# An MoE encoder block on one core: the branch on the round count is taken directly behind the routing index, ranks are computed one step later, and the final norm is regrouped

## The chip, the cores and the metric

One core of a Trainium2 chip. The metric is device time in microseconds (us), the median of several executions of the whole program; lower is better.

## The reference, cut to what matters

One encoder layer on 1024 tokens of width 1024, all in float32. The first half (norm, projections, differential attention, pooling, output projection) is not touched by the change. The second half is a mixture of experts: a router picks one group of four and two of its eight experts for every token, each of the 32 experts is a gated MLP, and the two weighted results of a token are added, scaled, added to the residual and normed.

```python
x = x + g1 * (mix @ w_out)
h = rms_norm(x, norm2_g) * (1 + sc2) + sh2
g_logits = h @ w_rg + b_rg;  g_sel = top-1 of 4;  g_p = softmax(g_logits)[g_sel]
e_prob = softmax((h @ w_re + b_re)[g_sel]);  top_p, top_i = top_k(e_prob, 2)
weights = g_p * top_p / sum(top_p);  expert_id = g_sel * 8 + top_i
for each expert e, on the tokens whose expert_id is e:
    hid = silu(xb @ w_gate[e]) * (xb @ w_up[e])       # 1024 -> 512
    y[token] += weight * (hid @ w_down[e])            # 512 -> 1024
x = x + g2 * y
return rms_norm(x, final_g)
```

Here 1024 tokens make 2048 assignments to 32 experts, and no expert receives more than 128 of them, so one block of 128 rows per expert is enough for these inputs. The kernel doesn't know this ahead: it counts.

## The kernel before, in words

Tokens are held in T = 8 tiles of 128 rows, one row per partition. Engines work from queues of their own, in program order: what is written earlier in the code for an engine runs earlier, and a waiting instruction holds up all that stands behind it on its engine. SP's queue holds most DMA issues.

**Router steps.** A loop over t = 0 to 8 computes the second part of the output projection of tile t (`out_products`, tiles `pm_0`, and `out_part(t, 4)`, tile `pm_4`; DVE adds both to the residual tile x), and the router of tile t - 1 (`flip` transposes x, `norm2_out` makes the normed rows `xn`, `router` the logits in `plg`). Routing works on batches of tiles (`BATCH`: tiles 0 to 2, 3 and 4, 5 to 7 are batches 0, 1, 2) and is a chain of small DVE instructions, cut in pieces. The tables `PLAN` (behind step t) and `LAST` (behind the loop) say where the pieces stand: `r` one step of `route`, `v` its rest (the weights), `k` `rank` (PE: matmuls `pR` on the one-hot `ob` and its running sums `cums`; DVE: the one-hot slot tiles `pk`), `p` `place` (PE: matmuls `lists`), `n` the norm of the last tile, `w` warm-up matmuls. `EARLY` issues 18 weight loads ahead of the branch, one tile of 128x1024 each.

```python
PLAN = {3: "r0 r0", 4: "r0 v0 k0", 5: "p0 r1 r1", 6: "r1 v1 k1"}
LAST = "p1 w10 r2 n7 r2 r2 k2 w4 p2"
```

**Between router and experts.** DVE turns `lists` into the index `ix`; POOL gathers the rows of the first two experts by it into `XG` (tiles x). `weights()` then finishes the weights of batch 2 (`v2`), places them (`place_weights`, matmuls `wlist`, copied to `LV`), counts the assignments of each expert (`pn`), and DVE makes of the largest the number of extra rounds `nri`. Every engine loads `nri` into a register (`nc.values_load`) and branches over a loop of extra rounds, which is skipped here. `warm2(n)` issues n transposes of the identity on PE whose result nobody reads; two instructions each.

**Experts.** The sequence `seq` holds 32 experts x 12 weight tiles. Each tile is loaded by SP (`w_next`), split by `we_split` into a high part `wh` (ACT) and a low part `wl` (DVE), and used by PE in six matmuls (`pg`, `pu` of the hidden layer, `py` of the result). `AHEAD` = 4 splits run ahead; the first four stand in front of the branch: two in step t = 7, two behind the gathers. `make_x(0, ...)` transposes the gathered rows of the first expert (`px`) and splits them into `xs`, high part on ACT and low part on DVE. ACT needs the table of Silu for the hidden layer (`hx`); it was on another table for Exp.

**End.** The results of the experts are scattered to `yd` in DRAM; SP loads them back as two rows per token (`fy`). `first_sum` adds these two, on DVE for tiles 0 and 1, on POOL for 2 to 7. Then for each tile: PE makes `yp` (sum, and the last expert's rows by a one-hot product; three buffers), DVE multiplies by `g2B` and adds the residual `xf`, ACT squares, POOL makes the reciprocal root `frs`, and DVE scales by it and by the norm row `fgB` (16 matmul rows on PE), and SP stores the tile.

Of the kernel before, what the change touches and what calls it, by code (L numbers as in the profile page):

```python
# [9 lines left out]
F32 = mybir.dt.float32  # L10
# [33 lines left out]
FILL = range(33, 41)  # L44
LOAD_RATE = 2
BATCH = [0, 0, 0, 1, 1, 2, 2, 2]
PLAN = {3: "r0 r0", 4: "r0 v0 k0", 5: "p0 r1 r1", 6: "r1 v1 k1"}
LAST = "p1 w10 r2 n7 r2 r2 k2 w4 p2"
EARLY = {4: 6, 5: 2, 6: 4, 7: 6}
ROWS = [5, 8, 11, 13]  # L50
MODS = {0: 1, 1: 2, 2: 2, **{m: 3 for m in range(3, 12)}}
# [16 lines left out]
def block_kernel(ctx: ExitStack, tc: tile.TileContext, A):  # L68
# [175 lines left out]
    with tc.tile_pool(name="ps0", bufs=2, space=PSUM) as psum, tc.tile_pool(name="ps1", bufs=2, space=PSUM) as psum1, \  # L244
# [790 lines left out]
                    pe.matmul(lists, PK[:, t, k], MV[:, t, k, 0:2].rearrange("p a b -> p (a b)"),  # L1035
                              start=(t0 + t + k == 0), stop=(t0 + t + k == T))

        def place_weights():
            p = pw("wlist", (NE,))
            for c in MVS:  # L1040
                PK, MV = MVS[c]
                t0, nt = RT[c][2:]
                for t in range(nt):
                    for k in range(2):
                        pe.matmul(p, PK[:, t, k], MV[:, t, k, 2], start=(t0 + t + k == 0), stop=(t0 + t + k == T))
                args = mvd[t0:t0 + nt].rearrange("t p k a e -> p t k a e"), MV
                if t0 + nt < T:
                    dma(*args)
                else:
                    stores.append(args)  # L1050
            return p

        pwarm2 = []

        def warm2(n):

# [10 lines left out]
        def plan(what):  # L1067
            for x in what.split():
                c = int(x[1:])
                if x[0] == "r":  # L1070
                    if c not in steps:
                        steps[c] = route(c)
                    next(steps[c], 1)
                elif x[0] == "v":
                    for _ in steps[c]:
                        pass
                elif x[0] == "n":
                    norm2_shift(c, XN.pop(c))
                elif x[0] == "k":
                    rank(c)  # L1080
                elif x[0] == "w":
                    warm2(c)
                else:
                    place(c)

        for t in range(T + 1):
            if t < T:
                out_products(t, 0, (0,))
            if t >= 1:
                flip(t - 1, 0)  # L1090
                flip(t - 1, 1)
                norm2_out(t - 1)
            if t < T:
                out_products(t, 0, (1,))
                out_add(t, 0)
            if t >= 1:
                router(t - 1)
            if t < T - 1:
                out_part(t, 4)
                norm2(t)  # L1100
            elif t == T - 1:
                for g in range(2):
                    we_split(*seq[g])
                out_part(t, 4, (0,))
                out_part(t, 4, (1,))
                norm2(t)
            for _ in range(EARLY.get(t, 0)):
                w_next()
            plan(PLAN.get(t, ""))
        plan(LAST)  # L1110

        dve.tensor_scalar(ix, lists.rearrange("p (a b) -> p a b", a=2), FAR, None, op0=OP.add)
        warm2(9)

        def weights():

            plan("v2")
            dve.tensor_copy(LV, place_weights())
            pn = pw("pn", (NE,))
            pe.matmul(pn, ones_b, cums[:, T], start=True, stop=True)  # L1120
            most = cst.tile([P, 2], F32, name="most")
            nri = cst.tile([P, 1], I32, name="nri")
            dve.tensor_reduce(most[:, 0:1], pn, axis=AX.X, op=OP.max)
            mj = cst.tile([P, 7], F32, name="mj")
            dve.tensor_scalar(mj, bounds, most[:, 0:1], None, op0=OP.is_lt, op1=OP.add, accum_out=most[:, 1:2])
            dve.tensor_copy(nri, most[:, 1:2])
            warm2(14)
            return nri

        XG = [X2[t] for t in (T - 2, T - 1)]  # L1130

        gather(XG[0], ix[:, 0, 0:1])
        gather(XG[1], ix[:, 0, 1:2])
        for g in range(2, AHEAD):
            we_split(*seq[g])
        nri = weights()
        pool_dma(*stores.pop())
        pins.clear()

# [63 lines left out]
    with tc.tile_pool(name="ps5", bufs=2, space=PSUM) as psum, tc.tile_pool(name="ps6", bufs=4, space=PSUM) as psum1:  # L1203
# [62 lines left out]
        def first_sum(t, eng):  # L1266
            eng.tensor_tensor(Y[2 * t], Y[2 * t], Y[2 * t + 1], op=OP.add)

        for step in (0, 2, 1, 3):
            make_x(0, step)  # L1270
        for g, (e, i) in enumerate(seq):
            while len(RW) < min(g + 1 + LOAD, len(seq)):
                w_next()
            if len(RW) == len(seq) and not XF:
                for t in range(T):
                    XF.append(slab(f"xf{t}"))
                    dma(XF[t], x2d[t * P:(t + 1) * P])
                G2.append(slab("g2B"))
                bcast_row(G2[0], rowd[3:4], D)
            if g + AHEAD < len(seq):  # L1280
                we_split(*seq[g + AHEAD])
            products(e, i)
            if i >= 8:
                e += 1
            j = i + 4 * (4 <= i < 8) - 4 * (i >= 8)
            if j == 0:
                if e > 0:
                    hidden(e - 1)
                if e + 2 < NE:
                    gather(XG[e % 2], ix[:, 0, e + 2:e + 3])  # L1290
            if j == HTJ and 0 < e < NE:
                hidden_t(e - 1)
            if j == 4 - (e == 0) and e < NE:
                HS[e] = ring("hx", 1, (512,))
                act.activation(HS[e], PG.pop(e), AF.Silu)
            if j == 8 and e > 0 or j == 7 and e == NE:
                y = ring("y", YN)
                act.activation(y, PY.pop(e - 1), AF.Copy, scale=LV[:, e - 1:e])
                if e < NE:
                    scatter(y, ix[:, 1, e - 1:e])  # L1300
                else:
                    ylast = y
            if (i, e) == (0, 2):
                zero = slab("zero")
                pool.memset(zero, 0.0)
                scatter(zero, ix[:, 1, NE - 1:NE])
            if (i, e) == (0, 3):

                OH.append(slab("onehot"))
                dve.tensor_copy(tlast, ix[:, 0, NE - 1:NE])  # L1310
                pool.iota(OH[0], pattern=[[1, S]], base=0, channel_multiplier=0, allow_small_or_imprecise_dtypes=True)
                pool.tensor_scalar(OH[0], OH[0], tlast, None, op0=OP.is_equal)
            if i == 4 and e == NE - 1:

                for t in range(T):
                    for k in range(2):
                        Y.append(slab(f"fy{t}_{k}"))
                        dma(Y[-1], yd.rearrange("(t k) d -> k t d", k=2)[k, t * P:(t + 1) * P])
            if i == 8 and e == NE:
                for t in range(2):  # L1320
                    first_sum(t, dve)
                for t in range(2, 5):
                    first_sum(t, pool)
            if j == 11 and e == NE - 1:
                hidden(e)
                hidden_t(e)
            if e + 1 < NE and j in (X_AT if e else X_AT0):
                make_x(e + 1, (X_AT if e else X_AT0)[j])
# [1 line left out]

    g2B = G2[0]
    psum = ctx.enter_context(tc.tile_pool(name="ps8", bufs=3, space=PSUM))
    fgB = rows(psum.tile([P, D], F32, name="fgB", bufs=1), fg)
    SS, RF, YP = {}, {}, {}
    for t in range(-1, T + 2):
        if 5 <= t + 4 < T:
            first_sum(t + 4, pool)
        if t + 1 < T:
            p = YP[t + 1] = psum.tile([P, 2, 512], F32, name=f"yp{t + 1}", tag="yp")
            for h in range(2):  # L1340
                cs = slice(h * 512, (h + 1) * 512)
                pe.matmul(p[:, h], ident, Y[2 * t + 2][:, cs], start=True, stop=False)
                pe.matmul(p[:, h], OH[0][:, (t + 1) * P:(t + 2) * P], ylast[:, cs], start=False, stop=True)
        if 0 <= t < T:
            y0, y1 = Y[2 * t:2 * t + 2]
            dve.tensor_tensor(y0, YP.pop(t).rearrange("p a b -> p (a b)"), g2B, op=OP.mult)
            dve.tensor_tensor(y0, y0, XF[t], op=OP.add)
            SS[t] = sm("fss", (1,))
            act.activation(y1, y0, AF.Square, accum_out=SS[t])
        if 0 <= t - 1 < T:  # L1350
            RF[t - 1] = sm("frs", (1,))
            rsqrt(RF[t - 1], SS[t - 1], 1, 1.0 / D, "fr")
        if 0 <= t - 2 < T:
            y0, y1 = Y[2 * t - 4:2 * t - 2]
            dve.scalar_tensor_tensor(y1, y0, RF[t - 2], fgB, op0=OP.mult, op1=OP.mult)
            dma(out[(t - 2) * P:(t - 1) * P], y1)

# [80 lines left out]
```

## Time and profile before

| | us |
|---|---|
| median of 3 runs (lowest to highest) | 1154.58 (1154.49 to 1155.22) |
| profiled execution, device time | 1156.02 |
| its span (first to last instruction) | 1154.2 |
| busy: PE, DVE, ACT, POOL | 1095.3, 971.5, 728.2, 248.6 |
| router steps t = 0 to 8 and placing, up to `ix` | about 444 to 519.5 |
| `ix` to the first matmul of the first expert | 519.5 to 534.4 |
| experts | 534.4 to 1108.2 |
| end | 1108.2 to 1154.2 |

Times of the stretches are of the profiled execution. A timeline row gives an instruction's (or a run of like instructions') start, length, engine, line, operation, output<-input, and in brackets the idle time of its engine ahead of it with what ended it. All helpers record their line as L81, so rows are told apart by the names of tiles.

### The profile page before, as it was taken

What the parts mean: (1) busy time and instruction counts of PE and PEld (TensorE: products, weight loads), DVE (VectorE), ACT (ScalarE), POOL (GpSimd) and SP (SyncE); (2) the same over time, 40 slices, a digit from 0 to 9 for tenths busy, and PEclk for the clock granted to TensorE, in tenths of its full rate; (3) what the DMA queues carried; (4) which work ended last, traced back from release to release, by engine and by line L of the source; (5) the groups of instructions that cost most, each with busy time, mean ns of one, the idle gap of its engine ahead of it and who ended that gap; (6) DMA issues with size and microseconds to landing.
All of it is one profiled execution on the core that took longest, in us unless ns stands there. A gap on an engine that the chain in (4) does not pass through costs nothing.

```text
span 1154.2 us, 15871 instructions
## 1 busy us (share of the span) xinstructions
PE 1095.3 (95%) x5379; PEld 899.1 (78%) x5379; DVE 971.5 (84%) x1232; ACT 728.2 (63%) x932; POOL 248.6 (22%) x197
## 2 busy tenths in 40 slices
PE   5898998999999999889999999999999999999984
PEld 5687787778888778778888888888888888888851
DVE  6977787689998766775999999999999999999957
ACT  6641232388877002224888888888888888888812
POOL 1000000178888011101131110110111101101042
PEclk9899999999999999978999999999999999999997
DMA  9949699696836435437999999999999999999473
GB/s 366 382 147 379 213 340 353 263 251 158 195 117 251 198 136 211 175 116 281 409 388 379 385 386 386 388 391 382 390 377 385 387 382 382 388 378 385 191 297 146
DMA packets 103719, 349.62 MB, mean 303 GB/s; under 512 B 16754, under 2 KB 17682, under 8 KB 103634
## 3 DMA queue, kind: packets, MB, share of 16 engines
q1 hardware_dynamic: 92034, 323.08, 76.3%
q0 software_dynamic: 11456, 24.96, 5.6%
q8 instruction: 43, 0.70, 0.3%
q10 hardware_dynamic: 144, 0.52, 0.1%
q14 instruction: 42, 0.34, 0.1%
HBM read 309.95 MB, written 55.33 MB: 316 GB/s over the span
## 4 chain that ended last, share of the span: by engine, by line
PE 48%; DVE 2%; issue 1%; DMA 1%; ACT 0%; SPq 0%; DVEq 0%; ACTq 0%
PE pg L81 28%; PE py L81 15%; PE px L81 2%; DVE fy L81 1%; PE pht L81 1%; DMA we<-in_w_exp 1%; PE yp L81 1%; DVE wl L81 1%; ACT wh L81 0%; SPq L102 0%; PE fgB L81 0%; ACT y L81 0%; DVE hx L81 0%; DVEq L1436 0%; ACT fy L81 0%
## 5 line engine op out<-in xcount | busy, mean ns | idle before, releaser
L81 DVE TENSOR_TENSOR wl<-we,wh 128x1024 fp32r<-128x1024 f32 x384 | 458.6, 1222 | 39.9 <-ACT wh L81 33.0
L81 ACT ACTIVATE wh<-we 128x1024 fp32r<-128x1024 f32 x384 | 399.9, 1059 | 58.7 <-PE pg L81 29.1
L81 PE MATMUL pg<-wh,xs 128*128 128x512 f32 x1024 | 338.7, 397 | 1.6 <-ACT xs L81 1.6
L81 PEld LDWEIGHTS pg<-wh,xs 128*128 128x128 f32 x1024 | 193.1, 189 | 40.5 <-ACT xs L81 1.8
L81 PE MATMUL pg<-wl,xs 128*128 128x512 f32 x512 | 200.3, 391 | 0.0
L81 PE MATMUL py<-wh,hth 128*128 128x512 f32 x512 | 172.3, 398 | 1.1 <-ACT hth L81 0.7
L81 POOL DMA_INDIRECT yd<-y,ix x31 | 30.8, 995 | 442.1 <-ACT y L81 441.8
L81 PEld LDWEIGHTS py<-wh,hth 128*128 128x128 f32 x512 | 96.8, 189 | 21.5 <-DVE hth L81 1.0
L81 PEld LDWEIGHTS pg<-wl,xs 128*128 128x128 f32 x512 | 96.8, 189 | 18.3
L81 PE MATMUL py<-wl,hth 128*128 128x512 f32 x256 | 100.5, 393 | 0.0
L81 ACT ACTIVATE e<-s,mx 128x1024 f32<-128x1024 f32 x64 | 71.8, 1121 | 28.8 <-DVE mx L81 25.1
L81 DVE TENSOR_REDUCE mx<-s 128x1 f32<-128x1024 f32 x64 | 78.2, 1222 | 6.0 <-PE s L81 3.2
L81 PE MATMUL s<-k,sq 128*128 128x512 f32 x256 | 72.6, 405 | 5.1 <-ACT e L81 5.0
L81 POOL TENSOR_TENSOR e<-e,e 128x1024 f32<-128x1024 f32 x32 | 76.6, 2393 | 2.7
L81 PE MATMUL po<-wh,v 128*128 128x256 f32 x256 | 60.8, 302 | 0.0
L81 POOL DMA_INDIRECT x<-xnd,ix x32 | 48.0, 1499 | 55.9 <-PE px L81 34.6
L81 DVE SCALAR_TENSOR_TENSOR wt<-wt,cB 128x1024 f32<-128x1024 f32 x48 | 56.3, 1219 | 0.8 <-ACT cB L81 0.8
L81 POOL TENSOR_SCALAR e<-e,cc 128x1024 f32<-128x1024 f32 x32 | 39.3, 1229 | 81.3 <-DVE cc L81 71.1
L81 PEld LDWEIGHTS py<-wl,hth 128*128 128x128 f32 x256 | 48.6, 190 | 9.5
L81 DVE SCALAR_TENSOR_TENSOR x<-pm,Y,x 128x1024 f32<-128x1024 f32 (+1 forms) x33 | 41.3, 1251 | 16.6 <-PE pm L81 15.5
L81 PEld LDWEIGHTS s<-k,sq 128*128 128x128 f32 x256 | 44.1, 189 | 13.8 <-ACT e L81 7.2
L81 ACT ACTIVATE xn<-x 128x1024 f32<-128x1024 f32 x7 | 7.4, 1061 | 70.4 <-DVE x L81 44.5
(246 smaller groups left out, 1864.7 us busy)
## 6 DMA issues: line engine op xcount, KB each, us to landing
we<-in_w_exp SPq DMA_DIRECT2D x384, 512.0 KB
wt<-in_w_ada SPq DMA_DIRECT2D x48, 512.0 KB
win<-in_w_in SPq DMA_DIRECT2D x16, 512.0 KB
woB<-wod SPq DMA_DIRECT2D x16, 512.0 KB
fy<-yd SPq DMA_DIRECT2D x16, 512.0 KB
k<-kd SPq DMA_DIRECT2D x32, 192.0 KB
xt<-in_xT SPq DMA_DIRECT2D x8, 512.0 KB
wo<-in_w_out SPq DMA_DIRECT2D x8, 512.0 KB
```

Source lines behind the costliest of these rows:

```text
L81: ins = getattr(self.eng, op)(*args, **kw)
```

## The change

Four things. (1) `PLAN` and `LAST`: `k0` moves from the end of step 4 to the head of what follows step 5, `p0` from there to step 6, `v1 k1` from the end of step 6 to step 7, ahead of `out_part(7, 4)`; there they take the place of the first two weight splits, which move to the ends of steps 5 and 6. The count `pn` (`c0`) stands ahead of `p2`. (2) The round count (`most`, `mj`, `nri`) stands directly behind `ix`; `v2`, the nine warm-up passes, `wlist` and `LV` follow, and then comes the branch. The fourteen warm-up passes behind `pn` are gone, and the third and fourth weight split stand behind the branch. (3) A Silu of one column (`tlast<-one`, overwritten later) stands behind the branch in the code. (4) End: DVE makes the first sums of tiles 0 to 3, POOL those of 4 to 7; `fgB` stands between `yp` of tiles 1 and 2; the last tile is scaled and stored in two halves, the second from ACT's queue.

```diff
-PLAN = {3: "r0 r0", 4: "r0 v0 k0", 5: "p0 r1 r1", 6: "r1 v1 k1"}
-LAST = "p1 w10 r2 n7 r2 r2 k2 w4 p2"
+PLAN = {3: "r0 r0", 4: "r0 v0", 5: "k0 r1", 6: "p0 r1 r1", 7: "v1 k1"}
+LAST = "p1 w10 r2 n7 r2 r2 k2 w4 c0 p2"
...
+                elif x[0] == "c":
+                    CP.append(pw("pn", (NE,)))
+                    pe.matmul(CP[0], ones_b, cums[:, T], start=True, stop=True)
...
             elif t == T - 1:
-                for g in range(2):
-                    we_split(*seq[g])
+                plan(PLAN[t])
                 out_part(t, 4, (0,))
                 out_part(t, 4, (1,))
                 norm2(t)
             for _ in range(EARLY.get(t, 0)):
                 w_next()
-            plan(PLAN.get(t, ""))
+            if t < T - 1:
+                plan(PLAN.get(t, ""))
+            if t in (5, 6):
+                we_split(*seq[t - 5])
         plan(LAST)
         dve.tensor_scalar(ix, lists.rearrange("p (a b) -> p a b", a=2), FAR, None, op0=OP.add)
-        warm2(9)
-        def weights():
-            plan("v2")
-            dve.tensor_copy(LV, place_weights())
-            pn = pw("pn", (NE,))
-            pe.matmul(pn, ones_b, cums[:, T], start=True, stop=True)
-            ...
-            warm2(14)
-            return nri
         XG = [X2[t] for t in (T - 2, T - 1)]
         gather(XG[0], ix[:, 0, 0:1])
         gather(XG[1], ix[:, 0, 1:2])
-        for g in range(2, AHEAD):
-            we_split(*seq[g])
-        nri = weights()
+        ...
+        dve.tensor_reduce(most[:, 0:1], CP[0], axis=AX.X, op=OP.max)
+        dve.tensor_scalar(mj, bounds, most[:, 0:1], None, op0=OP.is_lt, op1=OP.add, accum_out=most[:, 1:2])
+        dve.tensor_copy(nri, most[:, 1:2])
+        plan("v2")
+        warm2(9)
+        wl = pw("wlist", (NE,))
+        place_weights(wl)
+        dve.tensor_copy(LV, wl)
         pool_dma(*stores.pop())
...
+        act.activation(tlast, one, AF.Silu)
+        for g in range(2, AHEAD):
+            we_split(*seq[g])
         for step in (0, 2, 1, 3):
             make_x(0, step)
...
-                for t in range(2):
+                for t in range(3):
                     first_sum(t, dve)
-                for t in range(2, 5):
+                for t in range(4, 6):
                     first_sum(t, pool)
...
-    fgB = rows(psum.tile([P, D], F32, name="fgB", bufs=1), fg)
     for t in range(-1, T + 2):
-        if 5 <= t + 4 < T:
-            first_sum(t + 4, pool)
+        if t == -1:
+            first_sum(3, dve)
+        if 6 <= t + 5 < T:
+            first_sum(t + 5, pool)
...
+            if t == 0:
+                fgB = rows(psum.tile([P, D], F32, name="fgB", bufs=1), fg)
```

On DVE, between the index and the branch, the order before was as follows (`rt` and `mv` are the pieces of `v2`; `wl` are the third and fourth split; the last row loads the register that the branch reads):

```order
L81 TENSOR_SCALAR ix<-lists 128x64
L81 TENSOR_TENSOR wl_4646<-we_2_4215,wh_4645 128x1024
L81 TENSOR_TENSOR wl_4650<-we_3_4217,wh_4649 128x1024
L81 TENSOR_REDUCE rt_4399<-rt_4399 128x3 x2
...
L81 TENSOR_TENSOR mv<-rt_4399 128x6x32
L81 COPY LV<-wlist 128x32
L81 TENSOR_REDUCE most<-pn 128x1
L81 TENSOR_SCALAR mj,most<-bounds,most 128x7
L81 CAST nri<-most 128x1
L1141 TENSOR_LOAD nri
```

The same place on DVE now:

```order
L81 TENSOR_SCALAR ix<-lists 128x64
L81 TENSOR_REDUCE most<-pn 128x1
L81 TENSOR_SCALAR mj,most<-bounds,most 128x7
L81 CAST nri<-most 128x1
L81 TENSOR_REDUCE rt_4388<-rt_4388 128x3 x2
...
L81 TENSOR_TENSOR mv<-rt_4388 128x6x32
L81 COPY LV<-wlist 128x32
L1135 TENSOR_LOAD nri
```

The two splits went behind the branch, where they stand ahead of the two low parts `xs`; the count went ahead of `v2`.

On ACT, from the gathers' side of the branch to the first weight split of the stream, the order before was (rows of the skipped loop left out):

```order
L81 ACTIVATE wh_4645<-we_2_4215 128x1024
L81 ACTIVATE wh_4649<-we_3_4217 128x1024
L1141 TENSOR_LOAD nri
L1143 COMPARE_AND_BRANCH
...
L81 ACT_TABLE_LOAD
L81 ACTIVATE xs_4894<-px_0_4884 128x512
L81 ACTIVATE xs_4897<-px_1_4889 128x512
```

and it is now:

```order
L1135 TENSOR_LOAD nri
L81 ACT_TABLE_LOAD
L81 ACTIVATE tlast<-one 128x1
L1137 COMPARE_AND_BRANCH
...
L81 ACTIVATE wh_4863<-we_2_4215 128x1024
L81 ACTIVATE wh_4867<-we_3_4217 128x1024
L81 ACTIVATE xs_4881<-px_0_4871 128x512
L81 ACTIVATE xs_4884<-px_1_4876 128x512
```

The table load, with the one-column Silu, is now ahead of the branch instruction itself, although its line stands behind the branch in the code; two weight splits stand between the branch and `xs`. A second table load, ahead of the first `hx`, is gone too.

On DVE in steps 6 and 7 (`xn` the normed rows of tiles 5 and 6, `x` the residual adds of tile 7, `rt`, `mv`, `pk` the pieces of `v1` and `k1`) the end of the stretch is now:

```order
L81 TENSOR_TENSOR mv<-rt_4194,tok_104 128x4x64
L81 TENSOR_TENSOR wl_4437<-we_1_4213,wh_4436 128x1024
L81 SCALAR_TENSOR_TENSOR xn_4398<-x_3491,RS,gB 128x1024
L81 TENSOR_TENSOR xn_4398<-xn_4398,shB 128x1024
L81 TENSOR_TENSOR x_3493<-pm_0_4440,x_3493 128x1024
L81 SCALAR_TENSOR_TENSOR rt_4388<-plg,RS,rbias 128x36
L81 TENSOR_REDUCE rt_4194<-rt_4194 128x2 x2
...
L81 TENSOR_TENSOR pk_4499<-slots,RK 128x256 x2
L81 SCALAR_TENSOR_TENSOR x_3493<-pm_4_4509,Y_253,x_3493 128x512 x2
```

Before, `v1` and `k1` stood where the split `wl_4437` stands here, ahead of `xn`, and both first splits stood where `rt` to `pk` stand here.

## Rows read from the trace of the kernel before

**Rows 1.** Windows, expert stage: busy of each engine, granted clock, DMA share, GB/s.
```profile
559.00:584.00 25.00, 25.00 (x119) 20.73 (x118) 22.95 (x23) 21.82 (x24) 7.07 (x6) 1.00 1.02 406
```

**Rows 2.** Waits in 464.2 to 505: us in total, times, longest.
```profile
DVE x L81 <- PE pm L81: 9.0, 7, 2.7
...
PE pR L81 <- DVE ob L81: 3.9, 2, 2.0
...
DVE rt L81 <- PE plg L81: 1.4, 3, 0.5
```

**Rows 3.** Windows of DVE alone: busy, granted PE clock, DMA share, GB/s.
```profile
464.20:505.00 40.80, 29.35 (x75) 0.90 0.48 167
```

**Rows 4.** Timeline of DVE in steps 5 to 7.
```profile
476.82 1.28 DVE L81 SCALAR_TENSOR_TENSOR x<-pm,Y,x 128x1024 f32<-128x1024 f32 x1 [1.20 <-PE pm L81]
...
499.94 2.35 DVE L81 TENSOR_TENSOR wl<-we,wh 128x1024 fp32r<-128x1024 f32 x2
...
504.23 0.75 DVE L81 SCALAR_TENSOR_TENSOR x<-pm,Y,x 128x512 f32<-128x512 f32 x1 [1.28 <-PE pm L81]
```

**Rows 5.** Timeline of PE from the index to the first expert.
```profile
521.18 4.26 PE L81 MATMUL wlist<-mv,pk 128*128 128x32 f32 x32
...
525.30 6.02 PE L81 MATMUL pwarm<-ident 128*128 128x128 f32 x28
531.73 1.06 PE L81 MATMUL px<-ident,x 128*128 128x128 f32 x8 [0.40 <-PEq L1143]
534.37 0.79 PE L81 MATMUL pg<-wh,xs 128*128 128x512 f32 x1 [1.58 <-ACT xs L81]
...
535.39 1.05 PE L81 MATMUL pg<-wh,xs 128*128 128x512 f32 x2
```

**Rows 6.** Timeline of DVE over the same stretch.
```profile
525.47 0.19 DVE L81 COPY LV<-wlist 128x32 f32<-128x32 f32 x1 [2.24 <-PE pn L81]
...
526.06 0.15 DVE L81 CAST nri<-most 128x1 int32<-128x1 f32 x1
534.35 1.29 DVE L81 TENSOR_TENSOR xs<-px,xs 128x512 fp32r<-128x512 f32 x2 [8.13 <-ACT xs L81]
```

**Rows 7.** The branch's line: durations in ns, first and last start in us.
```profile
L1143 DVEq EVENT_SEMAPHORE  x1: 21/21/21, 527.1 to 527.1; - x1
...
L1143 PEldq EVENT_SEMAPHORE  x1: 51/51/51, 531.4 to 531.4; - x1
```

**Rows 8.** Timeline of ACT behind the branch.
```profile
532.42 1.28 ACT L81 ACT_TABLE_LOAD   x1 [17.07 <-PE px L81]
533.72 1.09 ACT L81 ACTIVATE xs<-px 128x512 fp32r<-128x512 f32 x2
```

**Rows 9.** DMA issues in 519 to 529: KB each, median us to landing.
```profile
x<-xnd,ix POOLq DMA_INDIRECT x2, 4.7
```

**Rows 10.** Timeline of POOL: first gather.
```profile
519.83 1.84 POOL L81 DMA_INDIRECT x<-xnd,ix  x1 [12.75 <-DVE ix L81]
```

**Rows 11.** Windows with the granted clock (third column from the right).
```profile
534.00:538.00 4.00, 3.63 (x9) 2.87 (x10) 2.52 (x3) 2.42 (x4) 0.11 (x1) 0.57 1.02 398
538.00:542.00 4.00, 4.00 (x20) 3.27 (x19) 3.03 (x3) 3.11 (x4) 0.00 (x0) 1.00 1.02 412
...
524.00:531.00 7.00, 7.00 (x36) 7.00 (x36) 0.67 (x5) 0.00 (x0) 0.37 (x1) 0.51 0.46 149
```

**Rows 12.** Timeline of the end: PE, POOL and DVE.
```profile
1109.39 2.05 PE L81 MATMUL fgB<-ident,cols 128*128 128x128 f32 x16 [1.20 <-ACT y L81]
...
1112.39 2.35 POOL L81 TENSOR_TENSOR fy<-fy,fy 128x1024 f32<-128x1024 f32 x1 [0.21 <-DMA fy<-yd]
...
1114.97 1.22 DVE L81 TENSOR_TENSOR fy<-yp,g2B 128x1024 f32<-128x1024 f32 x1 [6.53 <-PE yp L81]
1116.23 2.22 DVE L81 TENSOR_TENSOR fy<-fy,xf 128x1024 f32<-128x1024 f32 x1
...
1146.00 2.46 DVE L81 SCALAR_TENSOR_TENSOR fy<-fy,frs,fgB 128x1024 f32<-128x1024 f32 x2
```

More of the change, by code (lines that the diff above doesn't have):

```diff
@@ L1036, in place, with place_weights @@
                               start=(t0 + t + k == 0), stop=(t0 + t + k == T))
-        def place_weights():
-            p = pw("wlist", (NE,))
+        def place_weights(p):
             for c in MVS:
@@ L1050, in place_weights @@
                     stores.append(args)
-            return p
-        pwarm2 = []
+        pwarm2, CP = [], []
         def warm2(n):
@@ L1108, in block_kernel @@
                 w_next()
-            plan(PLAN.get(t, ""))
+            if t < T - 1:
+                plan(PLAN.get(t, ""))
+            if t in (5, 6):
+                we_split(*seq[t - 5])
         plan(LAST)
         dve.tensor_scalar(ix, lists.rearrange("p (a b) -> p a b", a=2), FAR, None, op0=OP.add)
-        warm2(9)
-        def weights():
-            plan("v2")
-            dve.tensor_copy(LV, place_weights())
-            pn = pw("pn", (NE,))
-            pe.matmul(pn, ones_b, cums[:, T], start=True, stop=True)
[L1121 to L1126, printed above, removed]
-            warm2(14)
-            return nri
         XG = [X2[t] for t in (T - 2, T - 1)]
@@ L1133, in block_kernel @@
         gather(XG[1], ix[:, 0, 1:2])
-        for g in range(2, AHEAD):
-            we_split(*seq[g])
-        nri = weights()
+        most = cst.tile([P, 2], F32, name="most")
+        nri = cst.tile([P, 1], I32, name="nri")
+        dve.tensor_reduce(most[:, 0:1], CP[0], axis=AX.X, op=OP.max)
+        mj = cst.tile([P, 7], F32, name="mj")
+        dve.tensor_scalar(mj, bounds, most[:, 0:1], None, op0=OP.is_lt, op1=OP.add, accum_out=most[:, 1:2])
[5 more added lines that the diff above has]
+        dve.tensor_copy(LV, wl)
         pool_dma(*stores.pop())
@@ L1354, in block_kernel @@
             y0, y1 = Y[2 * t - 4:2 * t - 2]
-            dve.scalar_tensor_tensor(y1, y0, RF[t - 2], fgB, op0=OP.mult, op1=OP.mult)
-            dma(out[(t - 2) * P:(t - 1) * P], y1)
+            for h in range(2 if t - 2 == T - 1 else 1):
+                cs = slice(h * 512, (h + 1) * 512) if t - 2 == T - 1 else slice(0, D)
+                dve.scalar_tensor_tensor(y1[:, cs], y0[:, cs], RF[t - 2], fgB[:, cs], op0=OP.mult, op1=OP.mult)
+                (act_dma if h else dma)(out[(t - 2) * P:(t - 1) * P, cs], y1[:, cs])
 def _layouts(inp):
```

## Prediction

> **What bounds the kernel now.** I read the windows of the expert stage first: a window of 25.00 us there has PE busy for 25.00 us at granted clock 1.00 [rows 1]. PE sets the pace from the first expert's matmul at 534.37 [rows 5] to the end of the experts, and 18 weight tiles lie loaded ahead of the branch by the table in the code. So whatever brings the first expert's matmuls forward brings the end forward by as much, and what happens on ACT, DVE or SP inside the experts is covered by PE. The change touches three stretches around this block: router steps, branch, end. They follow each other, so their terms add.
>
> In the router steps the waits tell who is late. Between 464.2 and 505 DVE is busy for 29.35 us of 40.80 [rows 3]; it waits 9.0 us in seven waits for PE's `pm`, and 1.4 us for `plg`. PE, in turn, stands still twice, 3.9 us in all, because `pR` needs `ob` of a routing step that DVE has only just begun [rows 2]. Neither engine is full: each waits for the other in turn.
>
> Around the branch the timelines show two late parties. DVE has copied `LV` at 525.66 and written `nri` at 526.21 [rows 6], and is through the branch at 527.1 [rows 7]. PE has 28 warm-up instructions queued, 6.02 us from 525.30 [rows 5], and passes only at 531.4 [rows 7]. Then `px`, a table load of 1.28 us on ACT ahead of `xs` [rows 8], the first expert's `pg` at 534.37, and its third matmul pair, the first that uses the low part of `xs`, at 535.39 [rows 5].
>
> **Router steps: 6.0 us.** No DVE instruction is added or dropped between the residual add of tile 4 and the last add of tile 7 (504.98 [rows 4]); they change places. What can shrink is the idle time, 40.80 - 29.35 = 11.45 us [rows 3]: 10.4 us of named waits [rows 2] and 1.05 us of gaps. With `k0` a step later, PE goes on with the matmuls of tile 5 while DVE finishes batch 0; with `k1` behind tile 6's products the same holds for batch 1. Walking DVE's new order by these durations, PE runs ahead of it nearly throughout, and these waits stay: the one for `pm` behind the router row of step 5, as at 476.82 (1.20); that for the second half of the last tile, as at 504.23 (1.28) [rows 4]; and a new one. The first weight split now stands behind routing steps whose Exp runs on ACT, and its `wl` has to wait until ACT has made `wh`: 1024 columns take 1.09 us there [rows 8], I take 1.35 us with the hand-over. With the gaps and 0.5 us for `plg` that leaves 1.20 + 1.28 + 1.35 + 1.05 + 0.5 = 5.4 us idle, so a gain of 6.0. Bounds: if all three `plg` waits (1.4) and one more wait of 1.20 stay, 4.0 (11.45 - 7.5); if the new wait and that for `plg` don't arise, 7.9. The moved splits (2.35 us for two [rows 4]) cost nothing extra, since they stand in the same stretch before and after. Behind 504.98 nothing but the count `pn` (one small matmul) is added up to `ix`, so the gain arrives there whole.
>
> **Branch: 5.5 us.** All times here are on before's clock. DVE now writes `nri` right behind `ix`, which nothing waits for; it then finishes `v2` without the two splits ahead of it. PE still does nine warm-up passes and `wlist`, until 525.44 [rows 5]: this set the time of `LV` before and does so now, so `LV` ends at 525.66. From its last instruction to passing, DVE took 527.1 - 526.21 = 0.9 us [rows 6, 7], so it is through at 526.55. PE has no warm-up passes left and is through earlier, but `px` waits for the others' release: about 526.75. ACT loaded its table ahead of the branch, where it idles for 17.07 us [rows 8], so `xs` starts 0.69 us behind `px` (532.42 - 531.73 [rows 5, 8]), at 527.45, and `pg` could start near 528.1. But DVE now has the third and fourth split first: 526.55 + 2.35 = 528.9 [rows 4], and half of 1.29 us [rows 6] for the low part of `xs`: 529.55. That is what the third pair waits for: about 529.65 to 529.9 instead of 535.39 [rows 5]. I take 5.5. So 1.5 us of what PE and ACT give free is spent on the two splits; if they found cover, the gain would be 7.0. The first gather is issued at 519.83 [rows 10] and lands 4.7 us later [rows 9], at 524.5, ahead of `px` by 2.2 us: the cover holds, but it was 7 us before. The low bound is 4.5, with 1 us lost to such landings. SP's weight loads restart earlier too; 18 loaded tiles cover them either way. The Silu's own column and the second table load cost PE nothing [rows 1].
>
> What the warm-up passes might have bought is the clock. Rows say: 0.51 in 524 to 531, while they ran, and 0.57 in 534 to 538, behind them; 1.00 from 538 [rows 11]. So the first expert started at half speed with them, and I charge nothing for their absence.
>
> The Trainium skill, "TensorE: Matmul & The Clock Gate", Part 1, says that the throttled state is the default and that activity releases it; by that, dropping the passes would cost the first expert clock. That speaks against this edit. Rows 11 show that the passes had not released it, and the effect is among the rivals below.
>
> **End: 0.75 us.** DVE sums tile 3 as soon as it lands (1112.39, where POOL's sum starts now [rows 12]) in about 1.2 us, and multiplies at 1113.6 instead of 1114.97, since PE's `yp0` no longer stands behind `fgB`'s 2.05 us [rows 12]. That is 1.3 us at best. Against it, the residual add takes 2.22 us while POOL adds [rows 12], and POOL still has four sums to do in that time; and `fgB` now delays `yp` of tile 2. I take 0.75, between 0 and 1.3. The halved last tile (the two last scalings take 2.46 us from 1146.00 [rows 12]) could bring its first half out by 0.6 us, but the store of tile 6 is ahead of it on the same DMA engines: 0 to 0.3, taken as 0.
>
> **Sum.** 6.0 + 5.5 + 0.75 = 12.25 us. Against the profiled execution: 1156.02 - 12.25 = 1143.8; it lies 1.44 above the median of the runs, so on that scale 1154.58 - 12.25 = 1142.3.
>
> **Rivals.**
> *A: the warm-up passes covered something that is now bare.* Behind PE's late pass at 531.4 any late arrival between 526.5 and 531 cost nothing: code of the block behind the branch, a landing, another engine's release. The nearest price for a fetch from memory is a DMA's 4.7 us [rows 9]. Then the branch gives 0.8 and the time is 1147.0. Against it: DVE's 0.9 us holds register load, comparison and jump [rows 6, 7], which leaves little for a stall.
>
> The Trainium skill, "Runtime: NRT & Kernel Launch", Instruction fetch mechanics, has the rule behind this: a taken branch to a page outside the two in the fetch window stalls until a DMA has brought it. By that rule each engine pays at the skipped loop; DVE's 0.9 us here shows no such stall, but PE's and ACT's could hide before 531.4.
>
> *B: the router is not freed.* If DVE's waits move to other partners (ACT's `wh` ahead of each `wl`, POOL's share of the norm), only about 2 us of the 11.45 go: 2 + 5.5 + 0.75, or 1146.3. For it: the seven waits for `pm` are spread over the stretch, the longest 2.7 us [rows 2], and are not only the sequel of two stops. Against it: a PE that never stops for `ob` is 3.9 us further on [rows 2] and has the products ready.
>
> *C: slower, by the clock.* If PE without the passes stays at half clock in the experts, each us so spent loses 0.5 us of work. The gain is gone once this lasts 24.5 us longer than before, and beyond 29 us the time is over 1156.9. Against it: PE is busy without a pause from 538 on and the clock came to 1.00 within 4 us of its start [rows 11]; PE will not be less busy then.
>
> *D: more than I count.* Splits under cover (7.0) and the router at 7.9: 1138.4.
>
> **How the numbers follow.** Forecast, 1140.2 to 1144.6 around 1142.3: 0.65. A (1144.6 to 1149): 0.13. B (1144.6 to 1148.3): 0.13. D: 0.05. C or an unseen loss: 0.04, most of it ending near no change. A measurement of this kernel can tell about 0.2%, 2.3 us, from no change. Faster by more than that: forecast, D and nearly all of A and B, 0.94; within: 0.03; slower: 0.03. The range takes in the forecast and most of A, B and D: 1139.5 to 1147.0.
>
> **What would show it.** Router right: the `pR` waits for `ob` gone, DVE idle in the stretch near 5.4 us, `wl` waiting once for `wh`. Branch right: PE passes near `wlist`'s end, no table load behind the branch, `pg`'s third pair some 10 us after `LV` was due to 4 us after, waiting for DVE's `xs`. End right: `fy<-yp` of tile 0 some 1.3 us earlier relative to ACT's last `y`. Wrong, if granted clock stays at 0.5 beyond the first 4 us of the experts, if `px` waits for its gather, or if DVE or ACT starts its first instruction behind the branch more than 1 us after its comparison.

## The result, and the profile after

| | us |
|---|---|
| changed kernel, median of 5 runs (lowest to highest) | 1146.33 (1144.31 to 1148.30) |
| ratio to the kernel before, with its 95% interval | 0.9924 [0.9903, 0.9945] |
| the same as a difference (of 1155) | 8.8 less (6.4 to 11.2) |
| profiled execution of the changed kernel: time, span | 1144.32, 1142.3 |
| predicted: median, range; on the profile's scale | 1142.3, 1139.5 to 1147.0; 1143.8 |

One of before's five runs beside these took 1245.93 us, where the others took 1154.49 to 1155.84; it is in a slow state and stands outside the ratio.

The time lies in the range and went the way that was forecast, but the gain is 8.8 us and not 12.25; the forecast's own band, 1140.2 to 1144.6, was missed. The two profiled executions alone differ by 1156.02 - 1144.32 = 11.7 us, almost as forecast. So the mechanism has to be looked for in the traces, and the missing 3.4 us in what the profile of before was.

The waits in the changed router steps, with the total, how often, and the longest:

```profile
DVE x L81 <- PE pm L81: 3.4, 3, 1.7
...
PE pm L81 <- DVE x L81: 3.2, 1, 3.2
...
DVE wl L81 <- ACT wh L81: 1.2, 1, 1.2
```

PE no longer waits for `ob` (3.9 us [rows 2]). DVE's waits for `pm` fell from 9.0 to 3.4 us, and the new wait for `wh` is there, once, with 1.2 us. One stop of PE stays, for DVE's first half of the last tile (`x`): 2.50 us before, 3.2 us now. DVE alone over the stretch, from the residual add of tile 4 to the end of tile 7's last add:

```profile
464.88:500.46 35.58, 30.02 (x75) 0.94 0.60 203
```

It is idle for 35.58 - 30.02 = 5.56 us; the prediction left 5.4. The parts differ more than the sum: the waits for `pm` are 3.4 us where it had 1.20 + 1.28, and none for `plg` falls into the stretch, where it had 0.5. From the index to the first expert, PE's timeline:

```profile
514.59 2.23 PE L81 MATMUL pwarm<-ident 128*128 128x128 f32 x18
516.65 3.78 PE L81 MATMUL wlist<-mv,pk 128*128 128x32 f32 x32
521.93 1.94 PE L81 MATMUL px<-ident,x 128*128 128x128 f32 x8 [1.50 <-DVEq L1137]
523.75 0.80 PE L81 MATMUL pg<-wh,xs 128*128 128x512 f32 x1
...
524.88 0.79 PE L81 MATMUL pg<-wh,xs 128*128 128x512 f32 x1
```

`px` starts 6.91 us behind the end of `ix` (515.02) where the prediction had 7.2, and the third pair 9.86 us, where it had 10.1 to 10.4; before it was 15.85 [rows 5]. The wait ahead of `px` is for DVE's way through the branch (duration in ns, first and last start in us):

```profile
L1137 PEldq EVENT_SEMAPHORE  x1: 51/51/51, 520.5 to 520.5; - x1
L1137 DVEq COMPARE_BRANCH  x1: 72/72/72, 521.1 to 521.1; - x1
L1137 DVEq EVENT_SEMAPHORE  x1: 21/21/21, 521.7 to 521.7; - x1
```

PE is through at 520.5, DVE at 521.7: `LV` ended at 520.66, so DVE needed 1.04 us (0.9 was reckoned). What differs from the plan is PE's speed: the eight `px` take 1.94 us where they took 1.06 [rows 5]. The windows show the clock that goes with it (granted clock in the third column from the right):

```profile
519.00:523.00 4.00, 2.50 (x17) 2.40 (x17) 1.33 (x2) 1.19 (x2) 0.00 (x0) 0.63 0.62 197
523.00:527.00 4.00, 4.00 (x12) 2.70 (x11) 3.65 (x5) 2.15 (x4) 1.04 (x1) 0.52 0.95 335
527.00:531.00 4.00, 4.00 (x19) 3.25 (x18) 2.58 (x3) 3.18 (x3) 0.00 (x0) 1.00 1.02 391
```

At the end DVE multiplies 4.27 us behind ACT's last `y` (1098.24) instead of 5.63, and pays part of it back at tile 2, behind the norm row:

```profile
1101.37 1.22 DVE L81 TENSOR_TENSOR fy<-fy,fy 128x1024 f32<-128x1024 f32 x1 [1.36 <-DMA fy<-yd]
1102.51 1.22 DVE L81 TENSOR_TENSOR fy<-yp,g2B 128x1024 f32<-128x1024 f32 x1
...
1110.68 1.22 DVE L81 TENSOR_TENSOR fy<-yp,g2B 128x1024 f32<-128x1024 f32 x1 [2.33 <-PE yp L81]
1111.94 1.96 DVE L81 TENSOR_TENSOR fy<-fy,xf 128x1024 f32<-128x1024 f32 x1
```

### The profile page after: what moved, and what is told of

Its sections match the earlier page's. It is cut to its first block, busy times and chain, and to the rows that moved or that the text cites. A ratio compares the mean times of both kernels' runs of the same rounds, so it can differ in the third digit from the quotient of the medians.

```text
span 1142.3 us, 15812 instructions
## 1 busy us (share of the span) xinstructions
PE 1091.3 (96%) x5351; PEld 895.7 (78%) x5351; DVE 971.2 (85%) x1235; ACT 726.7 (64%) x932; POOL 245.7 (22%) x195
## 4 chain that ended last, share of the span: by engine, by line
PE 49%; DVE 2%; DMA 2%; issue 0%; ACT 0%; POOL 0%; SPq 0%; DVEq 0%; ACTq 0%
PE pg L81 30%; PE py L81 15%; PE px L81 3%; DMA fy<-yd 2%; DVE fy L81 2%; PE pht L81 1%; DVE wl L81 0%; ACT wh L81 0%; SPq L102 0%; POOL frs L81 0%; ACT fy L81 0%; POOL fy L81 0%; DVEq L1440 0%; DVE hx L81 0%; ACT y L81 0%
## 5 line engine op out<-in xcount | busy, mean ns | idle before, releaser
L81 DVE SCALAR_TENSOR_TENSOR x<-pm,Y,x 128x1024 f32<-128x1024 f32 (+1 forms) x33 | 41.3, 1251 | 15.9 <-PE pm L81 14.8
```

Source lines behind the costliest of these rows:

```text
L81: ins = getattr(self.eng, op)(*args, **kw)
```

## The experiments

Two questions: does each of the three terms show when its part is built alone, and why is the measured gain smaller than the one between the two profiles? Theory 1 is the prediction's: three terms that add, sized as there. Its rivals in the first four runs are that a gain moves on into another wait, that missing passes cost clock, and that runs differ by the clock at the start (theory S). Theory L came out of these four: the old order's own length varies with the clock, and the profile of the prediction had the long ones. Each kernel left one more profile, and four stretches can be read in each from the timelines of DVE, PE and ACT: R, from the start of tile 4's last residual add to the end of tile 7's; B, from the end of `ix` to PE's third `pg` pair; X, from there to the end of ACT's last `y`; E, from there to the start of the two last scalings. "Start" is where R begins; all code ahead of it is the same in all kernels. From R's end to `ix` all kernels take 14.5 to 14.8 us.

| | start | R | B | X | E |
|---|---|---|---|---|---|
| before (profile of the prediction) | 463.00 | 41.98 | 15.85 | 573.95 | 36.66 |
| e9, before again | 466.76 | 40.15 | 13.93 | 572.97 | 36.94 |
| e1, router part alone | 463.35 | 35.58 | 13.93 | 572.91 | 36.13 |
| e2, branch part alone | 465.00 | 38.51 | 9.56 | 573.95 | 37.34 |
| e3, end part alone | 467.24 | 40.10 | 13.94 | 572.99 | 35.61 |
| e5, before, stops filled | 467.07 | 39.50 | 14.01 | 572.99 | 36.86 |
| changed kernel | 464.88 | 35.58 | 9.86 | 573.36 | 35.81 |
| e4, changed kernel again | 463.99 | 35.57 | 11.71 | 573.19 | 36.26 |
| e6, changed, fourteen passes back | 468.80 | 35.12 | 14.80 | 570.98 | 37.02 |
| e7, changed, splits ahead | 465.85 | 35.57 | 9.37 | 573.65 | 36.06 |
| e8, changed, no passes behind `ix` | 465.61 | 35.58 | 9.24 | 572.16 | 35.90 |
| e10, changed, no Silu | 465.50 | 35.58 | 9.80 | 574.50 | 35.93 |
| e11, e8 with another end | 464.17 | 35.58 | 8.81 | 572.78 | 36.20 |
| e12, e11 with splits ahead | 467.16 | 35.57 | 8.78 | 572.29 | 35.98 |

**e1: the router part alone.**

```diff
-PLAN = {3: "r0 r0", 4: "r0 v0 k0", 5: "p0 r1 r1", 6: "r1 v1 k1"}
+PLAN = {3: "r0 r0", 4: "r0 v0", 5: "k0 r1", 6: "p0 r1 r1", 7: "v1 k1"}
...
+                plan(PLAN[t])
...
+            if t in (5, 6):
+                we_split(*seq[t - 5])
```

> Before, with the table of steps of the change alone (ranks one step later, first two splits in steps 5 and 6). Theory 1 (the terms add, each as in the prediction): 6 us less than before; from the residual add of tile 4 to the end of the last add of tile 7 some 35.6 us instead of 41.98; the branch as before, with pg's third pair some 15.8 us behind the index. Theory 2 (the gain comes only because the later parts are also changed, and waits move on otherwise): under 3 us, with PE or DVE waiting longer between the last add of tile 7 and the index than the 14.56 us that both kernels took. If runs of one kernel differ by the clock at the start of the program, the profile's first 42 us show it.

Ratio 0.9951 [0.9928, 0.9973], 5.7 us less. R is 35.58, as theory 1 said and as in the whole change to 0.01 us; B is 13.93, which neither theory had (15.8): the branch of this kernel is that of before, word for word. So 15.85 wasn't the branch's own length. Theory 2 is out: from R's end to `ix` it takes 14.54 us, as before.

**e2: the branch part alone** (early count, `v2`, nine passes, `wlist`, `LV`, branch; splits and Silu behind it).

> Before, with the early round count, no fourteen warm-up passes, two splits and the Silu behind the branch; steps and end as before. Theory 1: 5.5 to 6 us less than before, pg's third pair some 9.9 us behind the index instead of 15.85, router steps as before (41.98 us). Theory 2 (without the passes the experts run longer at half clock): 2 to 4 us less, with granted clock near 0.5 in the experts for longer than the 3 to 4 us behind the first pg that before shows.

Ratio 0.9953 [0.9933, 0.9972], 5.4 us less. B is 9.56, near theory 1's 9.9. Theory 2's half clock is there, at 0.50 from 526.5 to 530.5, hardly longer than the 3 to 4 us that it allowed before. But R, the router of before, takes 38.51 instead of 41.98. PE's runs of twelve `pm` behind the two stops show where that comes from; in this kernel:

```profile
467.41 2.99 PE L81 MATMUL pm<-woB,mu 128*128 128x512 f32 x12
...
490.19 2.98 PE L81 MATMUL pm<-woB,mu 128*128 128x512 f32 x12
```

In the profile of before both took 4.6 us behind the same stops of 2.0 and 1.9 us; its timeline of PE:

```profile
465.42 4.58 PE L81 MATMUL pm<-woB,mu 128*128 128x512 f32 x12
...
489.80 4.60 PE L81 MATMUL pm<-woB,mu 128*128 128x512 f32 x12
```

The granted clock from 489.80 to 494.20 was 0.61 there. Over the four profiles with before's router (before, e2, e3, e9) four of eight such runs took 4.6 us and four 3.0; R is 38.51 with none, 40.10 and 40.15 with one, 41.98 with two. With the new order these two stops are gone, and R is 35.6 in every profile but e6 (35.1). Why the same stop has full clock behind it in one execution and half clock in another, the traces don't show.

**e3: the end alone.**

> Before, with the regrouped end alone. Theory 1: 0.5 to 1.2 us less, inside what times can tell; from ACT's last y to the last scaling 0.8 us less than before, because yp of tile 0 starts 2 us earlier and then yp of tile 2 waits for the norm row. Rival: POOL's sums delay DVE's residual adds as before, and nothing is gained (0 to 0.3 us).

Ratio 0.9996 [0.9973, 1.0018]: not to be told from before, as expected of 0.8 us. In the profile E is 35.61, below the 36.13 to 37.34 of the five with the old end. That speaks against the rival (nothing); the times don't rule it out.

**e4: the changed kernel again.**

> The changed kernel as it is. Theory 1: the sum of the three parts, some 11 to 12 us less than before; if single runs spread over 4 us again, theory S (start): the profile's first 42 us, which the change doesn't touch, show granted clock between 0.65 and 0.85 and explain the spread by up to 2 us. Rival: the spread arises in the branch or the experts' first us, and the runs of e1 and e3 have none of it.

1144.83 (1142.38 to 1147.84), ratio 0.9920 [0.9891, 0.9948]: 9.2 us. Theory S holds in part. Over 22 to 42 us, in code that the change doesn't touch, the granted clock is 0.67 in the first profile of the changed kernel and 0.82 here. The changed kernel:

```profile
22.00:42.00 20.00, 15.70 (x53) 12.31 (x53) 17.10 (x22) 12.81 (x17) 0.09 (x1) 0.67 1.03 409
```

and again (e4):

```profile
22.00:42.00 20.00, 14.48 (x60) 11.26 (x59) 18.37 (x24) 14.29 (x19) 0.00 (x0) 0.82 1.03 409
```

Here R starts 0.9 us earlier. Its rival holds as well: B is 11.71 instead of 9.86, since the nine passes ran at half clock this time. PE's timeline of e4:

```profile
513.77 4.00 PE L81 MATMUL pwarm<-ident 128*128 128x128 f32 x18
517.61 3.88 PE L81 MATMUL wlist<-mv,pk 128*128 128x32 f32 x32
523.00 1.94 PE L81 MATMUL px<-ident,x 128*128 128x128 f32 x8 [1.50 <-DVEq L1137]
```

**e5: before, with PE's two stops filled.**

```diff
+PLAN = {3: "r0 r0", 4: "w9 r0 v0 k0", 5: "p0 r1 r1", 6: "w9 r1 v1 k1"}
```

> Before, with nine warm-up passes on PE ahead of each of the first two ranks, where PE stands still for about 2 us. Theory L (the router's gain has a fixed part and one that hangs on the clock: behind a stop the twelve pm matmuls take 4.6 or 3.0 us, by execution): no stop, no slow run of twelve, and from the residual add of tile 4 to the end of tile 7's last add 38.5 to 39 us. Theory 1 (the stops themselves, each 2 us of idle PE, make the stretch long, whatever the clock): 41 to 42 us as in the profile of before, since the passes fill the time but DVE is as late as before.

Ratio 0.9981 [0.9960, 1.0002]. R is 39.50, between the two; theory 1's 41 to 42 is out, and neither dozen of `pm` takes 4.6 us:

```profile
466.87 2.17 PE L81 MATMUL pwarm<-ident 128*128 128x128 f32 x18
...
469.48 2.98 PE L81 MATMUL pm<-woB,mu 128*128 128x512 f32 x12
...
492.56 2.98 PE L81 MATMUL pm<-woB,mu 128*128 128x512 f32 x12
```

The 1.0 us over e2's 38.51 isn't spent on the passes: the first `pR` starts 1.97 us behind the start of R in both kernels. Some 0.3 us arise in step 6 between `lists` and `pm`, and 0.7 us at the last tile, where PE stops for DVE in every kernel and nothing was filled; the first matmuls behind that stop took 0.72 us in e2 and here

```profile
504.13 1.22 PE L81 MATMUL pm<-woB,mxh 128*128 128x512 f32 x2 [2.50 <-DVE x L81]
```

Since the twelve matmuls behind a stop took 4.6 us in half the cases only, two of 2.98 us prove little by themselves; they agree with theory L.

**e6: the changed kernel with the fourteen passes put back.**

```diff
         dve.tensor_copy(LV, wl)
+        warm2(14)
```

> The changed kernel with the fourteen warm-up passes put back behind the copy of the weights, ahead of the branch. If the passes cost what the prediction says and buy no clock: pg's third pair 3 to 6 us later behind the index than the 9.6 to 9.9 us (one profile: 11.7) without them, by the clock at which the passes run (28 instructions take 3.5 us at full and 6 us at half clock), and the experts behind it no shorter than 573 us from there to ACT's last y. Rival (they buy clock): the experts 1 to 2 us shorter, so that half of it comes back.

Ratio 0.9939 [0.9924, 0.9955], by time not to be told from the changed kernel. B is 14.80 and X is 570.98. PE's timeline of e6:

```profile
518.27 4.15 PE L81 MATMUL pwarm<-ident 128*128 128x128 f32 x18
...
526.06 5.00 PE L81 MATMUL pwarm<-ident 128*128 128x128 f32 x28
531.46 1.07 PE L81 MATMUL px<-ident,x 128*128 128x128 f32 x8 [0.41 <-PEq L1138]
532.83 0.53 PE L81 MATMUL pg<-wh,xs 128*128 128x512 f32 x1 [0.30 <-ACT xs L81]
```

The nine passes ahead of `wlist` took 4.15 us here, as in e4 (4.00) and not as in the first profile (2.23), so e4 is the one to compare with. Against it `px` starts 4.0 us later behind `ix`, and B is 3.1 us more. The rival's part is real: PE reaches `px` at full clock and needs 0.9 us less from there to the third pair, and behind it the first expert gives 0.8 us: its transposes `pht` start 15.63 us behind the third pair, in e4 16.44. The rest of the 2.2 us by which X is shorter than in e4 isn't the passes' work. It arises over 560 us later, at the last expert's `py`, behind two stops of PE that every kernel has. In e6 and, last row, in e4:

```profile
1096.04 0.66 PE L81 MATMUL pht<-ident,hx 128*128 128x128 f32 x4 [1.79 <-DVE hx L81]
...
1098.10 0.73 PE L81 MATMUL py<-wh,hth 128*128 128x512 f32 x2
...
1091.34 1.20 PE L81 MATMUL py<-wh,hth 128*128 128x512 f32 x2
```

From this `pht` to the end of the last `y` e6 takes 8.49 us, the thirteen other profiles 9.6 to 10.1. So between these two profiles the fourteen passes cost 4.0 us, and 1.7 us came back.

**e7: the two splits ahead of the branch.**

```diff
         plan("v2")
+        for g in range(2, AHEAD):
+            we_split(*seq[g])
         warm2(9)
...
-        for g in range(2, AHEAD):
-            we_split(*seq[g])
```

> The changed kernel with the third and fourth split ahead of the branch, behind the weights of batch 2, where DVE waits for wlist. Theory 1 (the two splits delay the low part of xs and with it pg's third pair by 1.5 us, as predicted): third pair 1.5 us earlier behind the index. Rival (px itself now waits, for DVE's pass or for its gather, and DVE has the splits done by then): 0 to 0.5 us.

Ratio 0.9930 [0.9909, 0.9951]. B is 9.37, 0.5 us less than 9.86 and 0.2 less than e2's 9.56: the rival holds. DVE's timeline of e7 shows that the low part of `xs` now waits for the high part; it starts 1.80 us behind `px` (522.50) instead of 2.21:

```profile
521.36 0.19 DVE L81 COPY LV<-wlist 128x32 f32<-128x32 f32 x1 [0.57 <-PE wlist L81]
524.30 1.50 DVE L81 TENSOR_TENSOR xs<-px,xs 128x512 fp32r<-128x512 f32 x2 [2.75 <-ACT xs L81]
```

**e8: no warm-up passes behind `ix`** (those in `LAST` stay).

```diff
         plan("v2")
-        warm2(9)
```

> The changed kernel without the nine passes ahead of wlist either. If wlist is on the path to the branch: px up to 2 us earlier behind the index (6.9 us before), as far as the first gather's landing (6.3 us behind its issue) lets it; so 0.2 to 0.5 us in a profile like the first, 2 us in one where the passes run at half clock. Rival (clock): wlist and px run at half clock all the time and the gain is lost, 0 or later by up to 1 us.

1143.66 (1142.75 to 1147.88), ratio 0.9916 [0.9890, 0.9941]. `px` starts 6.29 us behind `ix` instead of 6.91, and B and X together are 581.40, 1.8 us less than in the best profile of the changed kernel; 0.4 us of that arise only at the last expert's `py`. `px` doesn't wait for its gather, which landed at 520.45, 4.4 us behind its issue (the 6.3 us of the expectation are the second gather's). More isn't had, since the copy of the weights ends 1.8 us ahead of `px` (at 520.24) and DVE takes 1.07 us to load the register (the line's durations in ns):

```profile
L1134 DVEq TENSOR_LOAD <-nri x1: 1068/1068/1068, 520.1 to 520.1; - x1
```

**e9: before again.**

> The kernel before as it is, for another profile. Theory L (its router steps and its branch take longer or shorter by the clock behind PE's stops and under the warm-up passes, and the profile of the prediction had the slow case at each place): router steps (residual add of tile 4 to tile 7's last add) 38.5, 40.1 or 42.0 us, by none, one or two slow runs of twelve pm matmuls; index to pg's third pair 13.9 or 15.9 us. Theory 1: 42.0 and 15.9 again.

Ratio 1.0011 [0.9991, 1.0032]. R 40.15 and B 13.93: theory L, not theory 1. One of the two dozens of `pm` takes 4.6 us, the other 3.0. PE's timeline:

```profile
469.18 3.00 PE L81 MATMUL pm<-woB,mu 128*128 128x512 f32 x12
...
491.98 4.58 PE L81 MATMUL pm<-woB,mu 128*128 128x512 f32 x12
...
526.76 4.86 PE L81 MATMUL pwarm<-ident 128*128 128x128 f32 x28
...
534.67 0.50 PE L81 MATMUL pg<-wh,xs 128*128 128x512 f32 x1 [1.58 <-ACT xs L81]
```

and its window over the first expert, to be held against 0.57 in [rows 11]:

```profile
534.00:538.00 4.00, 3.33 (x13) 2.47 (x14) 2.79 (x4) 3.10 (x5) 0.41 (x1) 1.00 0.97 367
```

The 28 passes take 4.86 us here (6.02 in [rows 5]), and behind them the first expert runs at full clock.

**e10: no Silu ahead.**

```diff
-        act.activation(tlast, one, AF.Silu)
```

> The changed kernel without the Silu of one column, so that the tables are loaded by ACT behind the branch again, one ahead of the third split's wh and one ahead of the first hx. Theory 1 (the early load matters only if ACT is late for xs): 0 to 0.3 us, since ACT passes the branch about 4 us ahead of px and PE in the experts hides the other load. Rival (1.28 us stand on the path to xs or to hx, as before the change ahead of xs): pg 1.3 us later, or PE waits for hx.

Ratio 0.9946 [0.9931, 0.9962]. B is 9.80, as with the Silu: the first load stands under cover. The second, ahead of `hx`, does not. ACT's timeline of e10:

```profile
531.96 1.28 ACT L81 ACT_TABLE_LOAD   x1
533.25 0.60 ACT L81 ACTIVATE hx<-pg 128x512 f32<-128x512 f32 x1
```

and a wait of PE in the first expert's `py`, which before has too and the changed kernel hasn't:

```profile
PE py L81 <- DVE hth L81: 0.4, 1, 0.4
```

From the first expert's `pht` to the second's it takes 18.42 us here (542.49 to 560.91) and 17.74 in the changed kernel (541.40 to 559.14); all six profiles with the late load have 18.40 to 18.43, the eight with the early one 17.73 or 17.74. So the early table is worth 0.7 us on PE's path, over theory 1's 0 to 0.3 and, as the rival said, at `hx`. X is 1.1 us longer than in the changed kernel; the other 0.5 us arise ahead of that, with a granted clock of 0.80 over 527 to 531, where the changed kernel has 1.00.

**e11 and e12: both groups of passes behind `ix` gone, the norm row behind `yp` of tile 2, POOL's sums of tiles 6 and 7 a step later; e12 with the splits ahead as in e7.**

```diff
-        warm2(9)
...
-        if 6 <= t + 5 < T:
-            first_sum(t + 5, pool)
+        if 6 <= t + 4 < T:
+            first_sum(t + 4, pool)
...
-            if t == 0:
+            if t == 1:
                 fgB = rows(
```

> The changed kernel without the nine passes ahead of wlist, with the norm row behind yp of tile 2 instead of tile 1 and POOL's sums of tiles 6 and 7 one step later. If both hold: index to ACT's last y 581.4 us as in the kernel without the passes (583.2 to 584.9 in profiles of the changed one), from there to the last scaling 0.5 to 1.5 us less than the 35.8 to 36.3 of the changed kernel, because DVE no longer waits 2.3 us for yp of tile 2; together 2 to 4 us less. Rival for the end: the first reciprocal root and POOL's sums then set the pace, 0 to 0.5 us.

> The same as e11, and the third and fourth split ahead of the branch. If DVE's pass is what px waits for, the splits (2.4 us, the second waiting for ACT's wh) make the copy of the weights later and px up to 0.8 us later than in e11; if it is the gather, they cost nothing and the low part of xs is ready 0.3 us earlier.

e11: 1144.37 (1142.32 to 1145.63), ratio 0.9922 [0.9899, 0.9946]; e12: 1144.01, 0.9918 [0.9894, 0.9943]. By times neither is to be told from the changed kernel. By stretches B and X come out as expected (581.6 and 581.1 together, against 583.2 and 584.9), and the splits cost nothing. The end gives nothing: E is 36.20 and 35.98. DVE's timeline of e11 shows the wait at tile 2 shrunk to 0.39 us (1106.56, 10.66 us behind `y`; 12.44 in the changed kernel), and the gain handed back at tile 3's residual add:

```profile
1106.56 1.23 DVE L81 TENSOR_TENSOR fy<-yp,g2B 128x1024 f32<-128x1024 f32 x1 [0.39 <-PE yp L81]
...
1113.04 3.05 DVE L81 TENSOR_TENSOR fy<-fy,xf 128x1024 f32<-128x1024 f32 x1
```

It takes 3.05 us; the adds beside no sum of POOL's take 1.22 or 1.23. POOL is at its last sum then:

```profile
1112.67 2.34 POOL L81 TENSOR_TENSOR fy<-fy,fy 128x1024 f32<-128x1024 f32 x1
```

## Why the prediction was right in kind and too large in size

**Router steps, 6.0 us: right mechanism, mis-sized.** DVE's idle time came out near what was walked (5.56 against 5.4, in part by errors that cancel: PE's third stop, for the last half tile, was left out of the count and grew), and R fell by 6.4 us between the two profiles. The error is the minuend. The 11.45 us of idle time [rows 3] held two dozens of `pm` at 4.6 us instead of 3.0, and in the four profiles of the old order such are there in half the cases only. From 38.5 to 42.0, on average of four profiles 40.2, to 35.6 the term is 4.6 us, between 2.9 and 6.4.

**Branch, 5.5 us: one step failed.** "So the first expert started at half speed with them, and I charge nothing for their absence." One profile was taken for the rule, and only its mean over 524 to 531. Its own `px` took 1.06 us behind the passes [rows 5]; the granted clock, third from the right, was back at 1.00 there:

```profile
531.70:532.80 1.10, 1.06 (x8) 0.86 (x8) 0.00 (x0) 0.38 (x1) 0.00 (x0) 1.00 0.67 257
```

It fell to 0.50 (over 534.4 to 536.6) only after PE had waited 1.58 us for `xs`; in e9 it stayed at 1.00 behind the same wait. In e1, e6 and e9 the passes run at half clock at first, end at full clock, and `px` takes 1.07 us and `pg` starts at full speed; without them `px` takes 1.94 (in the changed kernel at 0.50, over 521.9 to 524) and the first 2 to 4 us of `pg` run at half clock. By e6 against e4 that costs 0.9 us up to the third pair and 0.8 us behind it. The rule of the Trainium skill that the prediction set against the row ("TensorE: Matmul & The Clock Gate", Part 1: throttled by default, activity releases it) agrees with these runs in kind.

B and X together are 586.8 to 587.0 in four profiles of the old branch (e1, e3, e5, e9) and 589.8 in that of the prediction; 583.2, 583.5 and 584.9 with the new one. The means, 587.5 and 583.9, give 3.6 us. So the new branch is as long as forecast (589.8 - 5.5 = 584.3); as in the router, the minuend was the long case. The passes still cost more than they gave.

Of its details, the way through the branch (1.04 us for DVE) and `pg`'s start were right within 0.4 us. That the second table load cost PE nothing was wrong (0.7 us, e10). The 1.5 us that the splits should cost were wrong too: e7 and e12 find 0 to 0.5; `px` and the first two `pg` at half clock take up most of that time. One sign of being wrong came up: ACT's first instruction behind the branch (`wh`, 518.18) starts 2.0 us after its comparison (516.2). ACT was at the table load and the Silu until 517.62; in e10, without the Silu, the next instruction starts 0.3 us after the comparison, so no stall of the branch shows.

**End, 0.75 us: right, as far as it can be told.** E is 36.8 on average of five profiles with the old end and 36.1 of seven with the new, or 35.9 without e6, whose `y` ended early: 0.7 to 0.9 us, where single profiles of one end differ by up to 1.4. Both signs came as argued, the start 1.4 us earlier and 2.3 us of wait behind the norm row.

**Sum.** 4.6 + 3.6 + 0.7 to 0.9 = 8.9 to 9.1 us, and 8.8 and 9.2 are measured. The sizes rest on the stretches of these few profiles. By their times the three parts alone gave 5.7, 5.4 and 0.5 us, 11.6 in sum, with some 2.5 us of interval to either side on each, which doesn't decide between 9 and 12. "1154.58 - 12.25" took off a median what only the profiled execution had to lose. That execution was 1.44 us above the median although it began its router steps at 463.00, the earliest start of all fourteen profiles: it had the long case at both stops and in the branch. The time of the changed kernel on the profile's scale, 1143.8, was met by its two profiled executions (1144.32 and 1145.63), although they began their router steps 1.9 and 1.0 us later than the profile of before; behind that start the first of them has 13.8 us less.

**Rivals.** A was wrong in the thing named (neither code nor a landing held PE up; DVE passed in 1.04 us), but the passes did cover something, the clock. B's 1146.3 is the measured time, and not for B's reason: the router was freed as planned. C's mechanism is real with about a tenth of its size: 2 to 4 us at half clock, not 24.5. That 1146.33 lies in the range is in part luck: the range reached up to 1147.0 for the sake of A and B, which didn't come about.

The first 463 us, which all kernels share, vary by 5.8 us, and the granted clock goes with them. In the six profiles with 1.00 over 100 to 200 us R begins at 463.0 to 465.0, in the eight with 0.98 at 465.5 to 468.8; e6, the latest, is also the only one with 0.99 over 200 to 300 us. What stays open is why the clock differs from execution to execution.

## What to carry to other kernels

A duration from one profile of a place where an engine has just stood still is one draw, not a price: look whether like instructions elsewhere in the same trace run faster, and size the gain from both. Taking a stop out of an order is worth twice, once for the stop and once because the length behind it no longer varies. Idle passes that only keep an engine warm are worth what they bring forward behind them less what they take; here 28 put the first expert off by 4.0 us and gave back 1.7.

## What the runs showed of the hardware that was not expected

- Behind a stop of PE of 2.0 or 1.9 us the same twelve matmuls took 3.0 us in four cases and 4.6 us in four. With the stop filled (e5) both runs took 2.98.
- Behind a stop of PE for `xs` of 1.58 us the granted clock was 0.50 in one profile of the old branch and 1.00 in another (e9); behind the last expert's stops, e6 alone of fourteen profiles ran at full clock throughout.
- The register load ahead of the branch took 0.46 to 0.69 us, and on DVE in the three kernels without passes behind `ix` (e8, e11, e12) 0.85 to 1.07 us; from DVE's comparison to its first semaphore behind the branch it took 0.2 us in before and 0.6 us in the changed kernel.
- POOL's sum of two tiles of 128x1024 takes 2.34 us and DVE's add of two such tiles 1.22 us where they don't meet. Where they do, DVE's took up to 3.05 us (e11) and POOL's up to 2.86 us (before, at 1117.81).
